# Nearest upsampling on one core: eight equal stores, three loads, and a load between two stores

## The chip, the cores and the metric

The kernel runs on one core of a Trainium2 chip. The metric is device time in microseconds (us) of one execution; lower is better. SP is the engine whose queue issues all transfers here, VectorE (DVE) and ScalarE (ACT) do the copies, and the transfers themselves run on the core's 16 DMA engines.

## The reference

The input x has shape (16, 64, 64, 64) in float32. Every pixel becomes a block of two by two:

```
result = zeros((16, 64, 128, 128))
for i in range(128):
    for j in range(128):
        result[:, :, i, j] = x[:, :, i // 2, j // 2]
```

16.78 MB are read and 67.11 MB written. There is no arithmetic, only copying.

## The kernel before, in words

The input is seen as 65,536 image rows of 64 floats. Each of the 128 partitions has 512 consecutive ones (R = 512). In memory on the chip an input row takes 64 floats of a partition; grown to its output it is 256 floats: each float doubled along the row (b), and the whole row written twice (a). In the main memory a partition's part of input and output is contiguous, so a transfer of k rows moves one run of bytes for each partition.

One tile, `mem`, holds everything. Its first `FREE` = 79 row groups are free space, the whole input stands behind them. Four loads (line 195) bring rows 0 to 32, 32 to 256, 256 to 480 and 480 to 512. All four are issued by SP; `begin_before_barrier` moves the first `EARLY` = 4 of SP's transfers ahead of the barrier with which the program starts.

Then nine stores follow, of 52, 40, 52, 63, 52, 64, 63, 63 and 63 rows. For each, VectorE copies the first 9/16 of its rows (line 215, an odd or an even number as it falls) and ScalarE the rest (line 216) into an expanded buffer, and SP stores it (line 217). The even ones (0, 2, 4, ...) have their buffer at the start of `mem`; the odd ones have it directly in front of the first input row that is still needed, over input that has been copied already. So a buffer is free again when the store before the last one has landed. Store 0 also waits, by a dependency added by hand, for the third load.

```
at = 0 if n % 2 == 0 else WF + r0 * W - size
kv = k * 9 // 16
nc.vector.tensor_copy(out=u[:, :kv], in_=expanded(r0, r0 + kv))
nc.scalar.copy(out=u[:, kv:], in_=expanded(r0 + kv, r0 + k))
store = nc.sync.dma_start(out=op[:, r0 : r0 + k, :], in_=u)
```

Order comes from semaphores that the tile framework places from reads and writes of `mem`. Each engine works off its queue in order; SP in particular issues a transfer only when all that stands ahead of it in its queue has been issued. A transfer that is issued is queued on the DMA engines behind those issued before it. `close_early` rearranges the end of the program, so that its last wait is the one for the last store; it is the same in both kernels.

Of the kernel before, what the change touches and what calls it, by code (L numbers as in the profile page):

```python
# [6 lines left out]

EARLY = 4  # L10


def begin_before_barrier(nc):
# [5 lines left out]
    sp = mybir.EngineType.SP  # L19
    loads = [i for i in body.instructions if i.engine == sp][:EARLY]  # L20
    for load in loads:
# [132 lines left out]
@with_exitstack  # L154
def kernel(
    ctx: ExitStack,
    tc: tile.TileContext,
    x: bass.AP,
    scale_factor: int,
    out: bass.AP,  # L160
):
    nc = tc.nc
    nc.at_finalize(begin_before_barrier)
    nc.at_finalize(close_early)
    P = nc.NUM_PARTITIONS
    s = int(scale_factor)
    B, C, H, W = x.shape
    R = B * C * H // P
    fdt = x.dtype

    xp = x.rearrange("b c h w -> (b c h) w").rearrange("(p r) w -> p r w", p=P)
    op = out.rearrange("b c (h hd) w -> (b c h) (hd w)", hd=s).rearrange(
        "(p r) w -> p r w", p=P
    )

    rows = [52, 40, 52, 63, 52, 64, 63, 63, 63]
    GROW = s * s
    FREE = 79
    WF = FREE * GROW * W
    assert sum(rows) == R
    mem_pool = ctx.enter_context(tc.tile_pool(name="mem", bufs=1))
    mem = mem_pool.tile([P, WF + R * W], fdt, name="mem")
    xt = mem[:, WF:].rearrange("p (r w) -> p r w", r=R)

    HEAD = 32
    cuts = [0, HEAD, R // 2, R - 32, R]
    loads = [
        nc.sync.dma_start(out=xt[:, lo:hi], in_=xp[:, lo:hi])  # L195
        for lo, hi in zip(cuts, cuts[1:])
    ]

    def expanded(r0, r1):
        return (  # L200
            xt[:, r0:r1].unsqueeze(2).unsqueeze(4).to_broadcast([P, r1 - r0, s, W, s])
        )

    r0 = 0
    before = (0, 0)
    for n, k in enumerate(rows):
        size = k * GROW * W
        at = 0 if n % 2 == 0 else WF + r0 * W - size
        assert at >= before[1] or at + size <= before[0]
        before = (at, at + size)  # L210
        u = mem[:, at : at + size].rearrange(
            "p (k a w b) -> p k a w b", k=k, a=s, w=W
        )
        kv = k * 9 // 16
        nc.vector.tensor_copy(out=u[:, :kv], in_=expanded(r0, r0 + kv))  # L215
        nc.scalar.copy(out=u[:, kv:], in_=expanded(r0 + kv, r0 + k))  # L216
        store = nc.sync.dma_start(out=op[:, r0 : r0 + k, :], in_=u)  # L217
        if n == 0:
            tc.add_manual_dep(
                store.ins,  # L220
                loads[-2].ins.name,
                mybir.DependencyInfo(
                    mybir.DependencyClass.Sync, mybir.DependencyReason.DATA
                ),
                reason="stores begin as the loads end",
            )
        r0 += k


# [33 lines left out]
```

## Time and profile before

| | |
|---|---|
| time, median of 3 runs | 196.99 us (196.85 to 197.22) |
| time of the profiled execution | 197.0 us |
| span in its profile, first to last instruction | 195.7 us |
| VectorE busy | 69.7 us, 9 copies |
| ScalarE busy | 51.4 us, 9 copies and a table load |
| DMA | 83.89 MB in 1872 packets, mean 429 GB/s over the span |
| transfers | 4 loads, 9 stores, all issued by SP |

The profile shows one execution. Its page gives the busy time of each engine; the span in 40 slices, each digit a slice's busy share in tenths; the DMA queues; the chain of work that ended last, followed back from the end; groups of instructions (line, engine, operation, tile written and read, shape, count, then busy time and mean ns of one, then idle time of the engine ahead of them and what ended it); and the transfers. In the chain in order of time a line is: start in us, duration in us, what. A transfer there is counted from its issue, or from the wait that it ended, to its landing, so it includes the time that it stood behind others in the queue. A packet is one run of bytes that one DMA engine moves; each transfer here has one for each partition, 8 on each of the 16 DMA engines, and an end marker on each.

### The profile page before, as it was taken

To read this page: it belongs to the slowest core of one execution; us is meant where nothing else is said; L and a number is where in the kernel's file an instruction comes from. 1 tells how busy PE (TensorE), PEld (TensorE's weight loads), DVE (VectorE), ACT (ScalarE), POOL (GpSimd) and SP (SyncE) were. 2 spreads that over 40 slices of the span, in tenths; PEclk is the share of its full clock that TensorE was granted. 3 is DMA by queue.
4 is the path that set the end of the run, shared out by engine and by line. 5 is a ranking of instruction groups with operands and counts; after the bars stand their busy time and mean duration, and the time that the engine had idled before them with its cause. 6 is when DMAs were issued, how large, how long until landed. Compare 5 with 4: busy or idle time off the path is not lost.

```text
span 195.7 us, 105 instructions
## 1 busy us (share of the span) xinstructions
DVE 69.7 (36%) x9; ACT 51.4 (26%) x10; POOL 0.2 (0%) x4
## 2 busy tenths in 40 slices
DVE  0950600000039299069008205930692079100000
ACT  0000595000036093064910006666000074000000
POOL 0000000000000000000000000000000000000000
DMA  9899889799899989899999899999999999999994
GB/s 402 375 481 457 375 375 563 310 440 523 348 442 452 526 348 512 359 422 422 422 422 523 348 523 429 429 429 429 422 422 422 422 422 422 528 514 422 435 422 211
DMA packets 1872, 83.89 MB, mean 429 GB/s; under 512 B 208, under 2 KB 208, under 8 KB 208
## 3 DMA queue, kind: packets, MB, share of 16 engines
q1 hardware_dynamic: 1872, 83.89, 99.3%
HBM read 16.78 MB, written 67.11 MB: 429 GB/s over the span
## 4 chain that ended last, share of the span: by engine, by line
DMA 67%; DVE 18%; SPq 0%; issue 0%; DVEq 0%
DMA out_dram<-mem 48%; DMA mem<-in_x_dram 19%; DVE mem L215 18%; SPq L195 0%; DVEq L215 0%; SPq L217 0%
## 5 line engine op out<-in xcount | busy, mean ns | idle before, releaser
L215 DVE COPY mem<-mem 128x8960 f32<-128x8960 f32 (+3 forms) x9 | 69.7, 7740 | 97.5 <-DMA out_dram<-mem 83.9
L216 ACT COPY mem<-mem 128x7168 f32<-128x7168 f32 (+2 forms) x9 | 50.1, 5572 | 90.8 <-DMA out_dram<-mem 84.3
L216 ACT ACT_TABLE_LOAD x1 | 1.3, 1283 | 21.6 <-DMA mem<-in_x_dram 21.6
L244 POOL MEMSET const-bfloat16-1.0<- 128x1 bf16 x1 | 0.1, 102 | 0.0
L244 POOL MEMSET const-uint8-127<- 128x1 uint8 x1 | 0.1, 102 | 0.0
L244 POOL MEMSET const-float32-0.0<- 128x1 f32 x1 | 0.1, 99 | 0.2 <-issue 0.2
L244 POOL MEMSET const-float32-1.0<- 128x1 f32 x1 | 0.1, 99 | 0.0
## 6 DMA issues: line engine op xcount, KB each, us to landing
out_dram<-mem SPq DMA_DIRECT2D x4, 8064.0 KB, 28.4
out_dram<-mem SPq DMA_DIRECT2D x3, 6656.0 KB, 19.7
mem<-in_x_dram SPq DMA_DIRECT2D x2, 7168.0 KB, 29.3
out_dram<-mem SPq DMA_DIRECT2D x1, 5120.0 KB, 29.8
mem<-in_x_dram SPq DMA_DIRECT2D x2, 1024.0 KB, 22.1
out_dram<-mem SPq DMA_DIRECT2D x1, 29.9
```

Of the source, the lines that this page charges most:

```text
L215: nc.vector.tensor_copy(out=u[:, :kv], in_=expanded(r0, r0 + kv))
L216: nc.scalar.copy(out=u[:, kv:], in_=expanded(r0 + kv, r0 + k))
L244: nc = _bacc.Bacc("TRN2", target_bir_lowering=False, num_devices=1)
```

## The change

The input no longer has a place of its own for all 512 rows. `mem` is laid out anew, in floats of a partition: 0 to 16384 is the buffer of store 0; from 16384 on (`xat`) stand input rows 0 to 319; from 36800 on (`high`) is the buffer of stores 1, 2, 4 and 6. Input rows 319 to 512 are loaded later, into the place where store 0's buffer was, 0 to 12352 (`low`), and the buffer of stores 3, 5 and 7 begins at `low`, over the rest of store 0's buffer and the input rows 0 to 193 that have been copied by then.

There are three loads: rows 0 to 64, rows 64 to 319 and rows 319 to 512. The first two are issued ahead of the barrier (`EARLY` = 2). The third is issued by SP between stores 1 and 2, and waits until store 0 has landed. The hand-made dependency of store 0 is gone.

All eight stores have 64 rows. VectorE copies 36 rows of each, but 61 of store 0 and 45 of store 2 (the first and the third); ScalarE has the rest. In store 3 the order of rows is ScalarE, VectorE, ScalarE: the last row's output covers the first row's input, and so it is copied last. The third load's first row (319) lies inside store 4, whose ScalarE part is split there.

In the compiled order of ScalarE the first part of store 3 (27 rows) stands ahead of its part of store 2 (19 rows); the first needs the landing of store 0, the second that of store 1. ScalarE's table load no longer waits for a transfer.

```diff
-EARLY = 4
+EARLY = 2
...
-    rows = [52, 40, 52, 63, 52, 64, 63, 63, 63]
     GROW = s * s
-    FREE = 79
-    WF = FREE * GROW * W
...
+    SHARE = {0: 61, 2: 45}
+    K = 64
+    FIRST = 319
+    U = K * GROW * W
+    xat = U
+    low, high = (R - FIRST) * W, xat + FIRST * W
...
-    HEAD = 32
-    cuts = [0, HEAD, R // 2, R - 32, R]
-    loads = [
-        nc.sync.dma_start(out=xt[:, lo:hi], in_=xp[:, lo:hi])
-        for lo, hi in zip(cuts, cuts[1:])
-    ]
...
+    def held(r0, r1):
+        at = (r0 - FIRST) * W if r0 >= FIRST else xat + r0 * W
+        assert r0 >= FIRST or r1 <= FIRST
+        return mem[:, at : at + (r1 - r0) * W].rearrange("p (r w) -> p r w", w=W)
+
+    def load(r0, r1):
+        nc.sync.dma_start(out=held(r0, r1), in_=xp[:, r0:r1])
+
+    def copy(engine, r0, r1, k0, at):
+        if r0 < FIRST < r1:
+            copy(engine, r0, FIRST, k0, at)
+            copy(engine, FIRST, r1, k0, at)
+            return
+        to = at + (r0 - k0) * GROW * W
+        u = mem[:, to : to + (r1 - r0) * GROW * W].rearrange(
+            "p (k a w b) -> p k a w b", a=s, w=W, b=s
         )
...
+        (nc.vector.tensor_copy if engine == "v" else nc.scalar.copy)(out=u, in_=v)
+
+    load(0, K)
+    load(K, FIRST)
+    for n in range(R // K):
+        k0 = n * K
+        at = 0 if n == 0 else high if n in (1, 2) or n % 2 == 0 else low
+        if n == 2:
+            load(FIRST, R)
+        nv = SHARE.get(n, 36)
+        if n == 3:
+            copy("s", k0, k0 + K - 1 - nv, k0, at)
+            copy("v", k0 + K - 1 - nv, k0 + K - 1, k0, at)
+            copy("s", k0 + K - 1, k0 + K, k0, at)
+        else:
+            copy("v", k0, k0 + nv, k0, at)
+            copy("s", k0 + nv, k0 + K, k0, at)
+        nc.sync.dma_start(out=op[:, k0 : k0 + K, :], in_=mem[:, at : at + U])
```

More of the change, by code (lines that the diff above doesn't have):

```diff
@@ L176 @@
     )
-    rows = [52, 40, 52, 63, 52, 64, 63, 63, 63]
     GROW = s * s
-    FREE = 79
-    WF = FREE * GROW * W
-    assert sum(rows) == R
-    mem_pool = ctx.enter_context(tc.tile_pool(name="mem", bufs=1))
-    mem = mem_pool.tile([P, WF + R * W], fdt, name="mem")
-    xt = mem[:, WF:].rearrange("p (r w) -> p r w", r=R)
-    HEAD = 32
-    cuts = [0, HEAD, R // 2, R - 32, R]
-    loads = [
-        nc.sync.dma_start(out=xt[:, lo:hi], in_=xp[:, lo:hi])
-        for lo, hi in zip(cuts, cuts[1:])
-    ]
@@ L199, in expanded @@
-    def expanded(r0, r1):
-        return (
-            xt[:, r0:r1].unsqueeze(2).unsqueeze(4).to_broadcast([P, r1 - r0, s, W, s])
-        )
[L204 to L212, printed above, removed]
-        )
[L214 to L227, printed above, removed]
+    SHARE = {0: 61, 2: 45}
@@ new lines @@
+    K = 64
[3 more added lines that the diff above has]
+    low, high = (R - FIRST) * W, xat + FIRST * W
+    assert R % K == 0 and low <= U
+    mem_pool = ctx.enter_context(tc.tile_pool(name="mem", bufs=1))
+    mem = mem_pool.tile([P, high + U], fdt, name="mem")
+    def held(r0, r1):
[4 more added lines that the diff above has]
+        nc.sync.dma_start(out=held(r0, r1), in_=xp[:, r0:r1])
@@ new lines, in copy @@
+    def copy(engine, r0, r1, k0, at):
[6 more added lines that the diff above has]
+            "p (k a w b) -> p k a w b", a=s, w=W, b=s
+        )
+        v = (
+            held(r0, r1)
+            .unsqueeze(2)
+            .unsqueeze(4)
+            .to_broadcast([P, r1 - r0, s, W, s])
+        )
+        (nc.vector.tensor_copy if engine == "v" else nc.scalar.copy)(out=u, in_=v)
```

## The prediction

> **What bounds the kernel now.** I read the page's first three parts, then the chain that ended last in order of time, then the groups by shape, and last the timeline for the start of single copies.
>
> ```profile
> span 195.7 us, 105 instructions
> ...
> DVE 69.7 (36%) x9; ACT 51.4 (26%) x10; POOL 0.2 (0%) x4
> ...
> DMA  9899889799899989899999899999999999999994
> ...
> q1 hardware_dynamic: 1872, 83.89, 99.3%
> ```
>
> The two copying engines are idle most of the time, and the one DMA queue is not: its packets fill 99.3% of the time of the 16 DMA engines. The bytes (16.78 MB in, 67.11 MB out) are fixed by the task, and the change moves the same ones. So the first question is at what rate the queue drains, and whether it ever runs dry. The chain answers both, since it gives the landings of single transfers.
>
> ```profile
> 0.91 37.52 DMA mem<-in_x_dram
> ...
> 38.52 18.23 DMA out_dram<-mem
> ...
> 56.85 7.90 DVE mem L215
> ...
> 64.83 19.72 DMA out_dram<-mem
> ...
> 92.60 26.66 DMA out_dram<-mem
> ...
> 128.95 28.65 DMA out_dram<-mem
> ```
>
> Start plus duration are landings: the third load at 38.43, store 0 at 56.75, store 2 at 84.55, store 4 at 119.26, store 6 at 157.60; the last store lands at the span's end, 195.6. Between them lie 92, 115, 127 and 126 output row groups of 131,072 bytes (one input row in every partition, grown fourfold). In us: 27.80, 34.71, 38.34, 38.0. That is 0.3018 to 0.3022 us for one, 434 GB/s, in each stretch, however the copies between them lie. The chain names DVE for 18% of the span, but these copies run beside the store that is draining: the queue had already been handed the next one. Nothing is lost there. The loads run at the same pace: the second load (7.34 MB) releases VectorE's second copy at 21.52 us, the first load its first copy at 4.59 us, 16.93 us apart, 434 GB/s.
>
> So the kernel is one transfer queue that drains at a fixed rate from about 1 us to the end. At that rate 83.89 MB take 193.3 us; the span has only 2.4 us beside it, the start and the last landing. A change can gain a part of these, or lose whatever it lets the queue idle.
>
> **The sum, part by part.** All times are on the profiled execution's own clock: 197.0 us, of which the span is 195.7 and 1.3 lies outside; the median of the runs is 196.99, so the two can be set equal.
>
> First the drain, step by step. The first load grows from 32 to 64 rows per partition (2.10 MB): 32 rows were there at 4.59, 32 more take 1.05 MB / 434 GB/s = 2.42, so about 7.0. The second load, 255 rows (8.36 MB), takes 19.26: 26.25. Each store has 64 groups, 19.33 us by the stretches above: store 0 ends at 45.6, store 1 at 64.9. The third load, 193 rows (6.32 MB), 14.57: 79.5. Six stores of 19.33: 195.5. Against 195.6 that is a gain of 0.1 to 0.15. It is the work of fewer pieces: 11 transfers in place of 13, and 1408 packets of data in place of 1664. The packet records of this trace say the same from below: a packet of 8,192 bytes takes 309 ns and one of 65,536 bytes 2,418, so 7 to 8 ns of each do not depend on size; 16 fewer on each DMA engine are 0.12 us, and two fewer end markers of 9 ns 0.02.
>
> Here a rule speaks for far more. The Trainium skill, "DMA: Bandwidth & Descriptors", in its section on the anatomy of one DMA, gives every transfer about 2.0 us on top of its bytes at 436 GB/s (fitted on transfers that GpSimd issued; here SP issues them). By it two transfers fewer would save 4 us (an estimate from that page), and two 63-group stores could not land 38.0 us apart, as they do here; the trace shows that a transfer queued behind another pays no such sum, and the measurement decides.
>
> Next, whether the queue is fed in time. The shapes give VectorE two rates:
>
> ```profile
> L215 DVE COPY mem<-mem 128x8960 f32<-128x8960 f32 x4 | 37.9, 9486 | 34.3 <-DMA out_dram<-mem 34.3
> L216 ACT COPY mem<-mem 128x7168 f32<-128x7168 f32 x5 | 30.8, 6164 | 56.5 <-DMA out_dram<-mem 50.1 <-DVE mem L215 6.4
> L215 DVE COPY mem<-mem 128x7424 f32<-128x7424 f32 x3 | 23.7, 7886 | 43.0 <-DMA out_dram<-mem 38.4 <-DMA mem<-in_x_dram 4.6
> ...
> L215 DVE COPY mem<-mem 128x9216 f32<-128x9216 f32 x1 | 5.0, 4960 | 11.2 <-DMA out_dram<-mem 11.2
> ...
> L215 DVE COPY mem<-mem 128x5632 f32<-128x5632 f32 x1 | 3.1, 3094 | 9.0 <-DMA mem<-in_x_dram 9.0
> ```
>
> Copies of 35 and 29 input rows cost 1.042 ns for an element of the output (1600 ns for 1536 elements), copies of 36 and 22 rows 0.521. The odd counts are the slow ones. The change gives VectorE 36 rows in six of eight stores (4.96 us each), and 61 and 45 in the first and third: odd, so by the slow rate 7.886 + 8192 x 1.042 ns = 16.4 us and 7.886 + 4096 x 1.042 ns = 12.15 us; by the fast rate they would be 8.3 and 6.2. I take the slow one. ScalarE's largest share, 28 rows, is a row of the trace (6.16 us).
>
> Store 0: VectorE starts at 7.0, ends at 23.4, and SP issues the store 0.08 later, 23.5 (in the chain a copy ends at 64.75 and its store is issued at 64.83). The second load lands at 26.25: a lead of 2.7 us. What is enough? In the kernel before, store 0 was issued at 38.52 while only the last 1.05 MB were queued, due at 40.85: a lead of 2.3 us, and store 0 landed at 56.75, its 15.7 us after 41.05. That is at most 0.2 us lost. From the first issue at 0.00 to the first packet the packet records have 1.02 us, and a landing is seen some 0.8 us after the first DMA engine has finished its part. So a lead under about 1.8 us would begin to cost.
>
> Stores 1 and 2 use the same buffer (high), so store 2 can only be copied when store 1 has landed, 64.9. This is the place that matters. SP has issued the third load before it, as soon as store 0 had landed (45.6), so the queue has 14.57 us of load to drain while VectorE copies 45 rows: start 65.0, end 77.15, issue 77.25. ScalarE's 19 rows are an easy 4.2 us; its 27 rows of store 3, ordered ahead on its queue, wait for store 0 alone and are done at 51.6. The load ends at 79.5: a lead of 2.25 us, close to the one the trace shows working, and 0.45 over what I reckon is needed. If the cover were gone, each us late would cost one. SP's queue holds no surprise: behind the third load's wait for store 0 stands only store 2, which is not ready for 31 us more.
>
> Stores 3 to 7 have about 13 us of cover: store 4's buffer is free when store 2 lands, near 98.8, its copies take 6.5, and store 3 drains until 118. The scattered small copies (ScalarE's single rows 319 and 255) lie inside this. So the copies cost nothing, and would cost nothing at either VectorE rate.
>
> Last, the third load adds a turn of the queue that the kernel before never makes: from writing to reading. Before shows the opposite turn, load to store, which lost at most the 0.2 us above; and reading from cold, where the first packets of the 16 DMA engines took 496 to 967 ns in place of 309, the second some 50 more: 0.5 us in all. So the turn costs between -0.05 (the overlap that store after store shows) and 0.5. Packets are queued ahead here, which is nearer to the first row: I take 0.15, and keep both ends.
>
> A rule speaks against the turn: the Trainium skill, "DMA: Bandwidth & Descriptors", section on latency and other measured facts, puts a memory access at 0.2 us on average and 2 us at high load. At high load the turn would cost nearer 2 us than 0.5 by it (an estimate from that page); no row of this trace shows a read under a write load.
>
> Sum: 197.0 - 0.13 + 0.15 = 197.0 us.
>
> **Rivals.** A measurement of this kernel can tell about 0.2%, 0.39 us, from no change.
>
> *The turn drains the pipe* (slower). At 64.9 us every DMA engine goes from store to load; if the first read's full latency is exposed, the load lands late and all six stores behind it move with it. The cold start's rows bound it: 0.5 us as the mean of the first packets, 1.7 us with the 1.02 from issue to first packet and the slowest packet's 0.66 on top. For it: nothing else in the queue can fill the hole. Against it: back-to-back transfers elsewhere show no hole. It decides from 0.52 us on (0.39 and the 0.13 gained): 197.4 to 198.6, and 197.6 at 0.7 us, nearer to the packets queued ahead.
>
> *Store 2 comes too late* (slower). The lead of 2.25 us rests on a 12.15 us copy that the trace does not hold, extended from 29 and 35 rows. If it is over 0.45 us longer than that, the queue runs dry near 79 us: a copy 1 us late costs 0.55 and a cold restart up to 0.5, 198.0 with the sum. Against it: the slow rate fits two shapes with the same slope.
>
> *The start gets cheaper* (faster). Before, the first and last loads have packets of 8 KB, and store 0's issue beside the last one cost up to 0.2. If larger packets remove the cold start's 0.5 as well, the time is 197.0 - 0.2 - 0.5 = 196.3. Against it: what is slow at the start is the first packet, of whatever size.
>
> That the change doesn't do what it says is only open for VectorE's odd rows: were they fast, the time stays 197.0, as the copies are covered.
>
> **The numbers.** No change that can be measured 0.70, the turn 0.13, store 2 late 0.09, the start 0.08. The forecast's own range is 196.8 to 197.4 (the turn's two ends); to hold 8 in 10 it is taken up into the milder slow cases, 196.7 to 197.7. Faster 0.08, same 0.70, slower 0.22.
>
> **What would show it.** The page: DMA share again about 99%, 1584 packets. The chain or the groups: a 128x15616 copy near 16.4 us and a 128x11520 copy near 12.15; landings of stores 19.33 us apart but for 34 us between stores 1 and 2. A dip of DMA near 65 us is the turn, one near 79 us the late store. The prediction is wrong if a stretch of stores alone runs at another rate than 434 GB/s, or if VectorE or ScalarE ends the chain's waits with the queue empty.

## The result, and the profile after

The changed kernel takes 199.10 us (median of 5 runs, 198.67 to 199.31), the kernel before beside it 197.04 us (196.85 to 197.22): a ratio of 1.0102, 95% interval 1.0088 to 1.0116. It is 2 us slower; 197.0 was forecast, with a range to 197.7. The profiled execution is the fastest of the five (198.67 us, span 197.3); the spans of the others are 197.7 to 198.0.

The page of the changed kernel, the parts that answer to those shown of before:

```profile
span 197.3 us, 98 instructions
...
DVE 58.3 (30%) x8; ACT 43.6 (22%) x11; POOL 0.2 (0%) x4
...
DMA  8999999999999999999999999999999999999994
GB/s 319 530 423 423 423 425 425 425 425 425 425 425 425 320 481 431 475 425 425 425 425 425 425 425 425 425 425 425 465 425 438 465 465 452 438 452 438 425 425 213
...
q1 hardware_dynamic: 1584, 83.89, 99.2%
```

The queue is still full, 99.2%. A packet that takes longer counts as busy all the same: this share can't show a loss of this kind. The GB/s row hints at it: mostly 425, and a dip to 320 in the 14th slice (64 to 69 us), where the queue goes from store 1 to the third load. It is no more than a hint, since the row of the kernel before dips as low with nothing lost:

```profile
GB/s 402 375 481 457 375 375 563 310 440 523 348 442 452 526 348 512 359 422 422 422 422 523 348 523 429 429 429 429 422 422 422 422 422 422 528 514 422 435 422 211
```

Landings place it. The timeline of the changed kernel (start, duration, engine, line, operation, idle time before and its releaser) has a copy that starts at each landing of a store:

```profile
45.92 5.95 ACT L215 COPY mem<-mem 128x6912 f32<-128x6912 f32 x1 [13.29 <-DMA out_dram<-mem]
66.88 4.68 ACT L215 COPY mem<-mem 128x4864 f32<-128x4864 f32 x2 [15.01 <-DMA out_dram<-mem]
66.93 17.22 DVE L215 COPY mem<-mem 128x11520 f32<-128x11520 f32 x2 [35.51 <-DMA out_dram<-mem]
79.17 86.12 SPq L232 DMA_DIRECT2D out_dram<-mem  x6
100.76 4.96 DVE L215 COPY mem<-mem 128x9216 f32<-128x9216 f32 x1 [16.61 <-DMA out_dram<-mem]
...
120.15 6.17 ACT L215 COPY mem<-mem 128x7168 f32<-128x7168 f32 x1 [13.08 <-DMA out_dram<-mem]
...
139.44 6.17 ACT L215 COPY mem<-mem 128x7168 f32<-128x7168 f32 x1 [13.12 <-DMA out_dram<-mem]
```

Stores 2, 3 and 4 land 19.3 us apart (100.76, 120.15, 139.44), as forecast. From store 0 to store 1 it is 20.96 in place of 19.33. From store 1 to store 2, with the third load between, it is 33.88, and 14.57 + 19.33 would be 33.90. So 1.63 us are lost, all of them before store 1 is seen to land.

The packet records say where. I take each packet's time above what is usual (the median) for its size, add up, and divide by the 16 DMA engines. In the changed kernel that is 0.55 us at the cold start (0.47 before), 0.09 on the second load's last packets, 0.60 on store 1's last packets (all 16 DMA engines, 2.8 to 3.4 us in place of 2.42), 0.92 on the third load's first packets, and nothing anywhere else. The late landing and the slow packets are one loss, not two: store 1's landings come on average 1.47 us after its last packets end, in place of 0.37 for store 0, and the load's slow first packets run in that time. The last store's landings, one for each DMA engine, lie 0.71 us apart in place of 0.42, and the span waits for the last of them: it comes 0.40 us after their mean, in place of 0.28.

### The profile page after: what moved, and what is told of

It reads as the page before. It is cut to its first block, busy times and chain, and to the rows that moved or that the text cites. A ratio compares the mean times of both kernels' runs of the same rounds, so it can differ in the third digit from the quotient of the medians.

```text
span 197.3 us, 98 instructions
## 1 busy us (share of the span) xinstructions
DVE 58.3 (30%) x8; ACT 43.6 (22%) x11; POOL 0.2 (0%) x4
## 3 DMA queue, kind: packets, MB, share of 16 engines
q1 hardware_dynamic: 1584, 83.89, 99.2%
## 4 chain that ended last, share of the span: by engine, by line
DMA 65%; ACT 9%; DVE 9%; issue 0%; SPq 0%; DVEq 0%; ACTq 0%
DMA out_dram<-mem 52%; DMA mem<-in_x_dram 13%; ACT mem L215 9%; DVE mem L215 9%; SPq L198 0%; DVEq L215 0%; ACTq L215 0%; SPq L232 0%
## 5 line engine op out<-in xcount | busy, mean ns | idle before, releaser
L215 DVE COPY mem<-mem 128x9216 f32<-128x9216 f32 (+2 forms) x8 | 58.3, 7292 | 105.4 <-DMA out_dram<-mem 95.3
L215 ACT COPY mem<-mem 128x7168 f32<-128x7168 f32 (+4 forms) x10 | 42.4, 4245 | 120.0 <-DMA out_dram<-mem 96.9
```

The source lines that it names most:

```text
L215: (nc.vector.tensor_copy if engine == "v" else nc.scalar.copy)(out=u, in_=v)
```

## The experiments

Theory A was that a turn of the queue between reading and writing main memory costs a fixed time. The rivals: the cost goes with the bytes (B), belongs to the layout or to the 64 KB transfers (C), or is a late store 2 (D).

**A turn put into the kernel before.** First a control: the hand-made dependency removed, so that store 0 is queued early. Then, on top of it, the last load held back; then two loads held back.

```diff
-        if n == 0:
-            tc.add_manual_dep(
-                store.ins,
-                loads[-2].ins.name,
...
```

> The control for the next two: the kernel before without the hand-made dependency, so that store 0 is issued as soon as it is copied (about 27 us), behind the third and fourth loads. All theories: the queue is full throughout, so the time is that of before within 0.2 us, about 197.0.

```diff
-EARLY = 4
+EARLY = 3
...
-        for lo, hi in zip(cuts, cuts[1:])
+        for lo, hi in zip(cuts[:-1], cuts[1:-1])
...
+        if n == 2:
+            nc.sync.dma_start(out=xt[:, R - 32 : R], in_=xp[:, R - 32 : R])
```

> The control with its last load (rows 480 to 512, 1.05 MB) moved behind store 2: same transfers, same bytes, one turn from store to load and one back. Theory A (each turn from store to load costs a fixed time, 1.5 us mean in the changed kernel's trace, whatever is loaded): 198.5. Rival B (the cost goes with the bytes loaded among stores, 1.5 us for 6.32 MB): 197.25. Rival C (the cost belongs to the new layout, or to the transfers of 64 KB, not to the turn): 197.0.

```diff
-    cuts = [0, HEAD, R // 2, R - 32, R]
+    cuts = [0, HEAD, R // 2, R - 64, R - 32, R]
...
-        for lo, hi in zip(cuts, cuts[1:])
+        for lo, hi in zip(cuts[:3], cuts[1:4])
...
+        if n in (2, 4):
+            lo = R - 64 if n == 2 else R - 32
+            nc.sync.dma_start(out=xt[:, lo : lo + 32], in_=xp[:, lo : lo + 32])
```

> The control with its last 64 rows held back as two loads of 32 rows, behind store 2 and behind store 4: one more load in number, two turns. Theory A: 2 x 1.5 us, 200.0. Rival B: 2.10 of 6.32 MB, 0.5 us, 197.5. Rival C: 197.0.

Measured against the kernel before (197.58 us): control 198.35 us, 1.0037 (1.0023 to 1.0050); one turn 199.68, 1.0103 (1.0089 to 1.0117); two turns 201.75, 1.0205 (1.0183 to 1.0227). One turn costs 1.3 us over the control and the second 2.1 more, where theory A had 1.5 for each and B 0.25. Only 1.05 MB were held back each time, and the layout stayed, as did the transfers' sizes in the run with one turn: B and C fall. Both costs are those of a load between two stores, from store to load and back again, as the next store is queued early here too.

The chains of the control (two lines) and of the run with one turn (two lines) show where the time goes:

```profile
28.29 29.82 DMA out_dram<-mem
...
66.17 19.72 DMA out_dram<-mem
```

```profile
28.26 27.47 DMA out_dram<-mem
...
63.80 20.76 DMA out_dram<-mem
```

Start plus duration are the landings of store 0 and store 2: 27.78 us apart in the control (58.11 to 85.89), 27.80 in the kernel before, 28.83 with the load queued behind store 2 (55.73 to 84.56). So 1.05 of the 1.3 us are lost before store 2 is seen to land. In the packet records this run loses less than the changed kernel, 0.53 on store 2's last packets and 0.24 on the short load; the rest of the 1.3 is that the last landing comes 0.91 us after the mean of the last store's landings, in place of 0.33 in the control.

The control was a miss, and the most useful one. It issues store 0 ten us earlier than the kernel before and loses 0.8 us.

Store 0 lands at 58.11; the third load had landed at 38.73, so 19.38 us lie between, where the kernel before has 18.32 (38.43 to 56.75) for the same bytes. The packet records put 1.08 us of excess on the fourth load's packets of 8,192 bytes, from 309 ns, the usual time, up to 1.05 us; in the kernel before, where store 0 is issued only at 38.52, those packets lose 0.01. So the turn from load to store costs too, here only where the store stands queued early.

**The same turn without reading main memory.** The changed kernel, its third load replaced by a transfer of the same shape within the chip's memory:

```diff
-            load(FIRST, R)
+            nc.sync.dma_start(out=mem[:, 0:low], in_=mem[:, high - low : high])
```

> The changed kernel with its third load replaced by a transfer of the same size inside the chip's own memory (rows 126 to 319 copied to where rows 319 to 512 belong; input rows 319 to 512 are not read, so the last three stores and a part of store 4 hold other rows). If what is slow is reading main memory behind stores (theory A1): the hole goes, and if the transfer runs at the 434 GB/s of the others the time is 199.1 - 1.5 = 197.6. If any change of direction on the DMA engines costs it (rival A2), or if store 2 is simply late (rival D): 199.1. If such a transfer runs at half the rate, 14.6 us are added to each, and the packets near 65 us tell.

Measured: 205.38 us, but the transfer itself is slower: its packets of 49,408 bytes take 2.82 us in place of 1.825. The timeline of this run, the copies that wait for store 0, store 1, and store 2:

```profile
46.07 5.95 ACT L215 COPY mem<-mem 128x6912 f32<-128x6912 f32 x1 [13.26 <-DMA out_dram<-mem]
65.34 4.24 ACT L215 COPY mem<-mem 128x4864 f32<-128x4864 f32 x1 [13.32 <-DMA out_dram<-mem]
...
106.98 4.96 DVE L215 COPY mem<-mem 128x9216 f32<-128x9216 f32 x1 [14.38 <-DMA out_dram<-mem]
```

Store 1 lands 19.27 us after store 0, not 20.96, and none of its packets takes over 2.43 us, though the next transfer was queued at 46.04, as early as in the changed kernel. The hole is gone; what is added (41.64 us from store 1 to store 2 in place of 33.88) is the transfer's own rate. With that rate put in, A1 gives about 205.5 (197.6 and eight packets on each DMA engine at 0.99 more) and A2 207.0. So a change of source alone doesn't cost it (rival A2 falls), and what is left is a read of main memory next to writes. One reserve: this transfer drains at two thirds of a load's rate, and no run has one at a load's rate.

**The two odd copies.** With theory A widened (either turn costs where the next transfer is queued early), VectorE's slow copies of 61 and 45 rows come into another light: they hold stores 0 and 2 back until the load ahead is nearly done. The changed kernel once more as control, and each of the two made short:

> The changed kernel once more, as the control of the next three on the same chip: 1.010 times the kernel before.

```diff
-    SHARE = {0: 61, 2: 45}
+    SHARE = {2: 45}
```

> The changed kernel with VectorE copying 36 rows of store 0 in place of 61. Store 0 is then issued near 13.3 us, 12 us before the second load's end, in place of 2.2. Theory A (any turn of the queue costs when the next transfer stands queued early; the control without the dependency lost 0.8 us so, from load to store): the last packets of the second load are stretched, 0.7 to 1.1 us slower than the changed kernel. Rival E (only turns from store to load cost; the control's loss has to do with 8 KB packets): the same as the changed kernel, within 0.2 us. The prediction's reading, that these copies cost nothing at either rate, is rival E too.

```diff
-    SHARE = {0: 61, 2: 45}
+    SHARE = {0: 61}
```

> The changed kernel with VectorE copying 36 rows of store 2 in place of 45 (both engines done about 6.2 us after store 1 has landed). Store 2 is issued near 73.2 us in place of 79.2, 7 us before the third load's end. Theory A: 0.7 to 1.1 us slower than the changed kernel. Rival E: the same. Rival D (in the changed kernel store 2 is issued too late, and the queue idles for it): faster by what it idles.

Measured against the kernel before (197.54 us): the changed kernel 199.23, 1.0087 (1.0071 to 1.0102); the first copy short 200.50, 1.0148 (1.0133 to 1.0163), 1.3 us slower than the changed kernel, a little more than the 0.7 to 1.1 that theory A had; the third short 199.89, 1.0122 (1.0105 to 1.0139), 0.7 slower. Both intervals lie clear of the control's, the second one narrowly: rival E falls, and D with it, since an earlier store 2 is no gain. Timeline of the run with the first copy short:

```profile
7.26 4.96 DVE L215 COPY mem<-mem 128x9216 f32<-128x9216 f32 x1 [7.26 <-DMA mem<-in_x_dram]
13.46 20.91 SPq L232 DMA_DIRECT2D out_dram<-mem  x2
27.83 4.96 DVE L215 COPY mem<-mem 128x9216 f32<-128x9216 f32 x1 [15.61 <-DMA mem<-in_x_dram]
```

The copy is done sooner and the store issued at 13.46 in place of 23.52; the second load then lands at 27.8 in place of 26.4. All 16 DMA engines' last packets of that load took 3.09 to 3.84 us in place of 2.41.

**The load queued late.** If early queueing is what costs, the turn from store to load should be cheaper with the load issued late. Eight copies by VectorE to a spare tile stand before it as a timer (`after` makes its first argument wait for its second):

```diff
-            load(FIRST, R)
+            x0 = xat + 200 * W
+            for t, size in enumerate([2048, 2048, 2048, 2048, 2048, 2048, 2048, 800]):
+                timer = nc.vector.tensor_copy(
+                    out=ps[:, :size], in_=mem[:, x0 : x0 + size]
+                )
+                if t == 0:
+                    after(timer, stores[0])
+            after(load(FIRST, R), timer)
```

> The changed kernel with its third load issued late: eight copies by VectorE to a spare tile, which start when store 0 has landed and end near 62.8 us, stand before it, so that it is issued about 2 us before store 1 has drained, in place of 19. Theory A: what the store's last packets lost (0.6 us) is not lost, and the load's first packets still lose between 0.5 (as from cold) and 0.9: 0.4 to 1.0 us faster than the changed kernel. Rival F (the turn from store to load costs the same whenever the load is queued, since a read behind stores waits anyway): the same as the changed kernel, or slower by what the queue idles.

Measured: 199.81 us, 1.0117 (1.0101 to 1.0132): no gain. Two lines of its timeline show why a first look would mislead:

```profile
65.76 17.22 DVE L228 COPY mem<-mem 128x11520 f32<-128x11520 f32 x2 [2.48 <-DMA out_dram<-mem]
77.99 88.61 SPq L253 DMA_DIRECT2D out_dram<-mem  x6
```

Store 1 now lands at 65.7, 0.4 us late in place of 1.6, and its packets lose nothing. But store 2 is so issued at 78.0, earlier than at 79.2, and the third load's last packets lose 0.34 us: the other turn again. So once more with that taken away, 49 rows of store 2 on VectorE:

```diff
-    SHARE = {0: 61, 2: 45}
+    SHARE = {0: 61, 2: 49}
```

> The kernel of the late third load, with 49 rows of store 2 on VectorE in place of 45. There store 2 was issued at 78.0, earlier than in the changed kernel as store 1 landed earlier, and the third load's last packets lost 0.34 us; 4 rows more make it 1.07 us later, 79.1, against a load that ends near 80.5. Theory A (a transfer queued early disturbs the one ahead of it): both losses gone, 0.3 to 0.6 us faster than the changed kernel, whose ratio to the kernel before is 1.0087 to 1.0102. Rival F (the turn costs the same whenever the load is queued): the same as the changed kernel.

Measured: 199.42 us against 197.66, 1.0092 (1.0078 to 1.0106): the changed kernel's time within the interval. Its timeline:

```profile
63.20 0.34 SPq L211 DMA_DIRECT2D mem<-in_x_dram  x1
...
65.80 18.28 DVE L228 COPY mem<-mem 128x12544 f32<-128x12544 f32 x2 [2.63 <-DMA out_dram<-mem]
79.10 86.70 SPq L253 DMA_DIRECT2D out_dram<-mem  x6
```

Store 1's packets lose nothing, the load's last ones nothing, but its first ones 1.32 us. Here theory A fails and rival F holds: queued late, the load takes nearly the whole loss itself. A gain of 0.6 us, theory A's upper end, is excluded; its lower end of 0.3 is not, as the two ratios of the changed kernel, 1.0087 and 1.0102, lie as far apart.

**Both turns in the kernel before.** An additional load of input rows 452 to 512, read a second time into free space:

```diff
+        if n == 5:
+            free = mem[:, 16384:WF].rearrange("p (r w) -> p r w", w=W)
+            nc.sync.dma_start(out=free, in_=xp[:, R - 60 : R])
```

> The kernel before with one more load, of input rows 452 to 512 once more (1.97 MB) into space that is free by then, between stores 5 and 6; both neighbours stand queued early. The bytes alone are 4.5 us at 434 GB/s. Theory A (store to load about 1.5 us, load to store with the store queued early about 1.0): 197.5 + 4.5 + 2.5 = 204.5. Only the turn from store to load costs: 203.5. The turns cost nothing in the kernel before, only in the new layout (rival C): 202.0.

Measured: 206.07 us against 197.66, 1.0415 (1.0389 to 1.0441): 8.4 us, of which 4.5 are bytes. The other 3.9 are more than the 2.5 that I had put together. The chain has store 4 and store 6:

```profile
92.94 26.81 DMA out_dram<-mem
...
129.41 36.99 DMA out_dram<-mem
```

They land 46.65 us apart (119.75 to 166.40) in place of 38.34, so nearly all of it lies there. Store 5's last packets lose 0.70, the load's own packets some 1.85, so 2.6 as a mean of the DMA engines; and the last store's landings now lie 2.3 us apart, in place of 0.42. The end waits for the slowest of them, 1.32 us after the mean in place of 0.28, which is 1.0 more. The remaining 0.3 no record explains.

The packet records side by side, in us as a mean of the 16 DMA engines; in the last two columns the landings of the last store, one for each DMA engine. For the added load's packets of 15,360 bytes 0.573 us is taken as usual, interpolated from 0.309 at 8,192 and 2.418 at 65,536 bytes, as most of them were slowed. The profiled execution with the third copy short was its slowest, 201.19 us where the median is 199.89, so that row is likely above the usual.

| kernel | end of the loads ahead of store 0 | end of the store ahead of the load | start of that load | end of that load | last landings apart | last one after their mean |
|---|---|---|---|---|---|---|
| before | 0.01 | none | none | none | 0.42 | 0.28 |
| dependency gone | 1.08 | none | none | none | 0.60 | 0.33 |
| one turn | 1.12 | 0.53 | 0.24 in all | | 1.47 | 0.91 |
| two turns, first | 1.16 | 0.56 | 0.26 in all | | | |
| two turns, second | | 0.71 | 0.21 in all | | 2.88 | 2.16 |
| load added to before | 0 | 0.70 | 1.85 in all | | 2.31 | 1.32 |
| changed | 0.09 | 0.60 | 0.92 | 0 | 0.71 | 0.40 |
| changed, again | 0.05 | 0.76 | 1.02 | 0 | 0.98 | 0.60 |
| first copy short | 1.18 | 1.05 | 0.76 | 0 | 0.79 | 0.62 |
| third copy short | 0.08 | 0.78 | 1.03 | 0.94 | 2.33 | 1.66 |
| load late | 0.01 | 0 | 1.15 | 0.34 | 1.63 | 1.00 |
| load late, 49 rows | 0.04 | 0 | 1.32 | 0 | 0.69 | 0.40 |

No run points to a version that beats the kernel before: it has the one turn that can't be avoided, from the last load to the first store, and its dependency already makes that one nearly free.

## Why the prediction was wrong

**What bounds the kernel**: right. Stores alone drain 64 groups in 19.32 us in both kernels.

**VectorE's rates**: right. The groups of the changed kernel by shape:

```profile
L215 DVE COPY mem<-mem 128x9216 f32<-128x9216 f32 x6 | 29.8, 4960 | 62.9 <-DMA out_dram<-mem 59.8 <-DMA mem<-in_x_dram 3.0
...
L215 DVE COPY mem<-mem 128x15616 f32<-128x15616 f32 x1 | 16.4, 16419 | 7.0 <-DMA mem<-in_x_dram 7.0
L215 DVE COPY mem<-mem 128x11520 f32<-128x11520 f32 x1 | 12.2, 12153 | 35.5 <-DMA out_dram<-mem 35.5
```

16.42 and 12.15 us, to the digits forecast from two odd shapes.

**Whether the queue is fed in time**: right. The chain of the changed kernel:

```profile
0.43 26.01 DMA mem<-in_x_dram
...
32.66 34.15 DMA out_dram<-mem
...
66.93 12.16 DVE mem L215
...
84.22 35.83 DMA out_dram<-mem
```

The second load lands at 26.44 (26.25 was forecast), store 0 was issued at 23.52 (23.5). Store 2 is issued at 79.17 against a load that lands at 81.4, a lead of 2.2 us as forecast, and it lands 19.33 us after it. The rival with the late store 2 is ruled out. The rival of the cheaper start is too: the cold start costs 0.55 us with the larger packets, 0.47 before.

**The turn from store to load**: this step failed. It was put at 0.15 us, between -0.05 and 0.5. The packets show 1.5 us in the profiled run and 1.8 in the next, three times the cold start that I took as its upper end. The error was the choice of row: a read from a queue at rest was let stand for a read behind full-rate writes, and then reduced because the packets are queued ahead; the late load shows that being queued 21 us ahead of store 1's landing gains nothing over 2.5. The Trainium skill's figure for a memory access at high load ("DMA: Bandwidth & Descriptors", "Latency and other measured facts"), by which the turn would cost nearer 2 us (an estimate), came nearer than my rows did; that the latency is the mechanism no run here shows. The rival that the turn drains the pipe had the right place and the right sign at 13%, with too low a price (197.6, at most 198.6). The sign that the prediction named for the turn, a dip of the DMA row near 65 us, did not come: that row stays at nine.

**The copies cost nothing at either rate**: wrong, and in an unexpected direction. More cover is not better: with the two odd copies made short the kernel loses 1.3 and 0.7 us, as the store behind a load is then queued too early. From this follows the second error in the turn: the 0.2 us of before for load to store, my lower row, is small only because its dependency issues store 0 late.

**The sum**: the medians lie 2.06 us apart, the spans of the two profiled executions 1.68 (195.67 and 197.34). The turn's packets explain 0.60 + 0.92 of this, the end of the second load 0.08, the cold start 0.08, the later last landing 0.12, and 0.13 go off for fewer pieces: 1.67. In the second profile of the changed kernel, 2.22 longer than before, it is 0.76 + 1.02 + 0.04 + 0.16 + 0.32 - 0.13 = 2.17. No run shows the 0.13 by itself. The later last landing stood in none of my terms.

**Open**: whether the reads wait in main memory or in the DMA engines' reading side, and why a store that is queued early disturbs the load ahead of it. The copy within the chip shows only that the hole goes when the next transfer doesn't read main memory, and that transfer was slower than a load.

## What to carry to other kernels

In a kernel that is one full transfer queue, count the turns between reading and writing main memory, not the transfers: here a load between two stores cost 1.3 to 2.1 us with 1.05 MB held back, about 2 in the changed kernel with 6.32 MB, where it made no difference whether the load was queued early or late, and 3.9 beyond its bytes when it was added to the kernel before; two transfers fewer bring 0.13 by the packet records (an estimate). For the turn from load to store, issue the store late, 2 to 3 us before the load ahead of it ends: 0.8 to 1.3 us were lost by queueing store 0 some 10 us earlier than that. And don't take a full DMA share for a queue at its full rate: compare landing intervals with the bytes between them.

## What was unexpected of the hardware

- A transfer queued long ahead, behind another of the other direction, slows the last packets of the one in front of it: load packets of 65,280 bytes took 3.09 to 3.84 us in place of 2.41 with a store queued, store packets of 65,536 bytes 2.8 to 3.4 in place of 2.42 with a load queued.
- A transfer within the chip's memory ran at 49,408 bytes in 2.82 us on each DMA engine, 280 GB/s over 16, while the same shape from main memory ran at 433.
- A store can be seen to land long after its last packets: 1.47 us on average for store 1, with a load behind it, and 0.36 for the same store with a copy within the chip behind it.
- After a turn the DMA engines drift apart, and do not come together again by the end: 0.42 us between their last landings before, 2.3 with a load that is disturbed at both ends. In the runs with 1.05 MB held back this drift is about half of the loss.
